# Experts in sorted order with 192, 128 or 64 slots, and 64-slot blocks whose high and low parts share one tile

## The chip, the cores and the metric

One core of one Trainium2 chip runs the whole program. The metric is device time in microseconds (us) of that core for one execution.

## The reference, cut to what matters

Two layers work on 256 latent tokens (and 256 context tokens) of 1024 channels. The second layer ends with a mixture of eight experts, and only that part is touched here:

```python
def moe_swiglu(h, router, w1, w3, w2):
    logits = (h @ router).astype(jnp.float32)
    top_v, top_i = lax.top_k(logits, TOP_K)            # 2 of 8
    top_w = jax.nn.softmax(top_v, axis=-1)
    ...
    out = comb[..., 0:1] * swiglu(h, w1[0], w3[0], w2[0])
    for e in range(1, N_EXPERTS):
        out = out + comb[..., e:e + 1] * swiglu(h, w1[e], w3[e], w2[e])
    return out

def swiglu(h, w1, w3, w2):
    return (jax.nn.silu(h @ w1) * (h @ w3)) @ w2
```

All is float32. w1 and w3 of an expert are 1024 x 3584, w2 is 3584 x 1024. Each of the 256 tokens goes to two experts, so the eight experts have 512 tokens in all. On the reference's default inputs the router gives them 39, 31, 9, 142, 44, 100, 55 and 92 tokens.

## The kernel before

**Precision.** The tensor engine's one-pass float32 format holds part of a float32 number. `split` (lines 116 to 124) makes of a tile a high part `h` (a cast on ScalarE, line 120) and the rest `lo` (a subtraction on VectorE, line 121); `mm3` (lines 126 to 130) then multiplies in three passes, high x high, high x low and low x high, which accumulate in PSUM.

**Positions.** `route` (lines 966 to 1091) finds the two experts of each token and the rank of each token within its expert. The expert with the most tokens is position 0 of an order, and the others follow cyclically by number (lines 1022 to 1040). Position 0 has 256 slots in two blocks, the seven others have one block of 128 slots. What is beyond 128 tokens of an expert other than position 0 is handled after the rest by overflow positions 8 and 9 (two at most), under a condition on the chip (lines 1297 to 1301).

**A block.** `gather` (lines 1093 to 1120) builds one-hot rows and takes the block's tokens with matmuls from `hm`, which holds the tokens split: result are two tiles `xg` (high and low), tokens as columns. Then come seven chunks of 512 hidden units. `up1` (line 1147) multiplies by a chunk of w1 and applies silu on ScalarE; `up3` (line 1154) multiplies by a chunk of w3, takes the product on VectorE (line 1159), transposes it with four matmuls against the identity (line 1162) and splits it (line 1164) into `gh` and `gl`; `down` (line 1168) multiplies these by the chunk of w2 and accumulates 128 x 1024 results `y`. The block of tokens is the stationary operand of all these matmuls, and 512 columns of weights move. `back` (line 1172) adds the block's results, weighted, to the rows of its tokens.

**Weights.** `mload` (line 1122) loads 1 MB of weights from SP's queue into one of five buffers `mland` and splits it in two pieces into `mwh` and `mwl` (eight buffers each). A chunk takes six such loads, an expert 42.

**Order.** `steps` (line 1211) runs positions 1 to 7, three steps a chunk: `up1`, the `down` of the chunk before, `up3`. The other generator, `steps0` (line 1248), runs both blocks of position 0 on the same weights, two steps a chunk: `up1`, and `up3` with `down`, whose results are added up in SBUF (lines 1264, 1266). `experts` (line 1269) interleaves them: after two steps of the first and then after every tenth, one of the 14 steps of position 0. The next position's gather is made at a position's chunk 5. A scheduler then puts the instructions of each engine in order, by priorities and its own estimate of times, so that matmuls of neighbouring steps can be mixed. PSUM has three banks for `mp` (and gathers and results), four for `y`, and one for transposes.

Of the kernel before, what the change touches and what calls it, by code (L numbers as in the profile page):

```python
# [10 lines left out]
FT = mybir.dt.float32  # L11
# [8 lines left out]
KD = 8  # L20
# [6 lines left out]
MAGIC = 12582912.0  # L27
INV2PI = 1.0 / (2.0 * math.pi)
# [17 lines left out]
def tables():  # L46
# [24 lines left out]
    for i in range(8):  # L71
        for tp in range(8):
            for ch in range(16):
# [3 lines left out]
                if k <= 0:  # L77
# [3 lines left out]
    c["moec"] = np.broadcast_to(np.concatenate([i8, np.mod(i8[None, :] - i8[:, None], 8).ravel(),  # L81
                                                np.arange(128)]).astype(f32), (128, 200)).copy()
# [5 lines left out]
class Net:  # L88
# [43 lines left out]
    def wchunk(self, src, n, tags=None):  # L132
        """One weight chunk of 512 KB, split: its n blocks of columns."""
# [66 lines left out]
    def s5_pre(self, l):  # L200
# [54 lines left out]
        for b in range(NB):  # L255
# [24 lines left out]
            def cmul(o, va, vb, vc, op1, eng):  # L280
                """(ar * va op0 ai * vb, ar * vc op1 ai * va), products over powers and channels."""
# [187 lines left out]
    def hy_filters(self, l):  # L469
        """Transforms of both orders' two-sided filters (over 256) to DRAM."""  # L470
# [62 lines left out]
    def hy_in(self, l, t0, part):  # L533
        """Short convolution of one part of the projection."""
# [15 lines left out]
    def hy_turn(self, q, s, out):  # L550
        """Token-major copy of a part of one sequence; two tiles get its split."""
# [11 lines left out]
    def hy_conv(self, kk, z, order, sink):  # L563
        """Long convolution of one sequence; sink takes each piece of the result."""
# [59 lines left out]
    def hy_second(self, l, z1, x1, seqs):  # L624
        """The second order; the result takes the place of x1."""
# [69 lines left out]
    def stats(self, x):  # L695
        """Mean, (var + eps)^-0.5 and -mean times that of the rows of a token tile."""
# [16 lines left out]
    def norm_affine(self, out, x, g, b):  # L713
        """Layer norm of a token tile with the rows g, b."""
# [12 lines left out]
    def modulate(self, xn, w, sh, sc):  # L727
        """Two normalized token tiles (w: context or latent) transposed, modulated and split into hh, hl."""
# [21 lines left out]
    def mods(self, l, part, tag="Y", fast=False):  # L750
        """Part 0..5 of the modulation (shift, scale, gate, twice) as columns [128, tile, (context, latent)]; the
# [779 lines left out]
```

## Time and profile before

| | |
|---|---|
| median of 3 runs | 2717.94 us (2716.2 to 2720.52) |
| profiled execution, first to last instruction (span) | 2714.0 us |
| mean granted TensorE clock over the span | 0.956 |
| tensor engine busy | 2542.4 us, 94% |
| VectorE, ScalarE, GpSimd busy | 2191.7, 1384.9, 191.3 us |
| DMA | 602.58 MB, mean 222 GB/s |
| expert stage | from about 1565 us to the end |

The profile was taken of one execution; its own time is known as its span, 2714.0 us, which is 3.9 us under the runs' median. Busy time of an engine is a share of the span over all stages. A matmul's shown duration includes its way through the array and overlaps those beside it; the distance between two starts is what it costs in a dense stream. The granted clock is that of the tensor engine, 1.00 being 2.4 GHz and 0.50 being 1.2 GHz.

### The profile page before, as it was taken

How to read it: one execution, taken by the hardware profiler on the slowest of the kernel's cores; microseconds unless marked ns; L12 is line 12 of the kernel's file. 1: busy time of each engine (PE TensorE's matmuls, PEld its weight loads, DVE VectorE, ACT ScalarE, POOL GpSimd, SP SyncE). 2: the span in 40 equal slices, each digit the busy share in tenths (PEclk: the TensorE clock that was granted, in tenths of full speed). 3: DMA queues.
4: the chain of work that ended last, by engine and by line, in shares of the span. 5: the costliest groups of instructions: out<-in, count | busy, mean ns of one | idle time of the engine just before them, and what ended most of it. 6: DMA issues, size and time to landing. Idle time of an engine off the chain costs nothing. (4 is left out here: it accounts for less than half of the span.)

```text
span 2714.0 us, 35372 instructions
## 1 busy us (share of the span) xinstructions
PE 2542.4 (94%) x12732; PEld 2117.1 (78%) x12732; DVE 2191.7 (81%) x3154; ACT 1384.9 (51%) x1891; POOL 191.3 (7%) x202
## 2 busy tenths in 40 slices
PE   7888999999899989969999799999999999999997
PEld 3766886788777878858999688888888888888875
DVE  8876799975769897566898787888878788888887
ACT  4344442333542323334445376777767676777764
POOL 2520010000100132110000100000000000000000
PEclk8988999999899989979899889999999999999998
DMA  6454444533235555545445288898889898898974
GB/s 254 152 190 152 144 126 168 179 130 113 79 126 189 179 187 170 189 149 187 152 148 175 89 328 307 324 342 310 329 292 332 295 334 302 322 337 318 334 270 177
DMA packets 147353, 602.58 MB, mean 222 GB/s; under 512 B 41878, under 2 KB 42584, under 8 KB 104160
## 3 DMA queue, kind: packets, MB, share of 16 engines
q1 hardware_dynamic: 147168, 600.23, 62.9%
q8 instruction: 102, 1.67, 0.2%
q14 instruction: 83, 0.68, 0.1%
HBM read 563.96 MB, written 36.21 MB: 221 GB/s over the span
## 5 line engine op out<-in xcount | busy, mean ns | idle before, releaser
L121 DVE TENSOR_TENSOR mwl<-mland,mwh 128x1024 fp32r<-128x1024 f32 x672 | 802.9, 1221 | 157.8 <-ACT mwh L120 133.4
L120 ACT CAST mwh<-mland 128x1024 fp32r<-128x1024 f32 x672 | 700.3, 1054 | 276.6 <-PE mp L130 188.9
L120 ACT CAST wh<-land 128x512 fp32r<-128x512 f32 x396 | 244.7, 621 | 527.7 <-PE p L129 242.0
L128 PE MATMUL mp<-mwh,xg 128*128 128x512 f32 x1008 | 395.7, 394 | 0.4 <-ACT xg L1113 0.4
L129 PE MATMUL mp<-mwl,xg 128*128 128x512 f32 x1008 | 395.2, 392 | 0.0
L130 PE MATMUL mp<-mwh,xg 128*128 128x512 f32 x1008 | 394.7, 392 | 0.0
L121 DVE TENSOR_TENSOR wl<-land,wh 128x512 fp32r<-128x512 f32 x396 | 285.0, 723 | 114.8 <-ACT wh L120 106.4
L128 PE MATMUL p<-hh,wh 128*128 128x256 f32 (+1 forms) x800 | 278.5, 349 | 14.2 <-DVE q L546 8.1
L130 PE MATMUL p<-hh,wl 128*128 128x256 f32 (+1 forms) x800 | 278.6, 350 | 4.6 <-DVE wl L121 3.9
L129 PE MATMUL p<-hl,wh 128*128 128x256 f32 (+1 forms) x800 | 276.0, 346 | 0.1
L130 PEld LDWEIGHTS mp<-mwh,xg 128*128 128x128 f32 x1008 | 189.9, 188 | 39.6
L128 PEld LDWEIGHTS mp<-mwh,xg 128*128 128x128 f32 x1008 | 189.9, 189 | 39.0 <-ACT xg L1113 0.5
L129 PEld LDWEIGHTS mp<-mwl,xg 128*128 128x128 f32 x1008 | 190.1, 189 | 38.4
L128 PE MATMUL y<-mwh,gh 128*128 128x512 f32 x504 | 195.9, 391 | 1.8 <-ACT gh L120 1.8
L129 PE MATMUL y<-mwl,gh 128*128 128x512 f32 x504 | 196.0, 390 | 0.0
L130 PE MATMUL y<-mwh,gl 128*128 128x512 f32 x504 | 190.1, 392 | 0.0
L128 PEld LDWEIGHTS p<-hh,wh 128*128 128x128 f32 x800 | 157.6, 197 | 34.4 <-issue 8.7
L784 DVE SCALAR_TENSOR_TENSOR ma<-mw,sv,ma 128x512 f32<-128x512 f32 x196 | 153.1, 804 | 37.0 <-DMA mw<-in_w_mod 36.5
L130 PEld LDWEIGHTS p<-hh,wl 128*128 128x128 f32 x800 | 157.3, 197 | 25.8 <-DVE wl L121 8.9
L129 PEld LDWEIGHTS p<-hl,wh 128*128 128x128 f32 x800 | 158.0, 198 | 15.9 <-DVE hl L748 0.3
L130 PE MATMUL fo<-hh,wl 128*128 128x512 f32 (+1 forms) x384 | 147.2, 384 | 2.7 <-DVE wl L121 2.7
L128 PE MATMUL fo<-hh,wh 128*128 128x512 f32 (+1 forms) x384 | 147.5, 385 | 1.4 <-ACT hh L744 0.9
(442 smaller groups left out, 4369.8 us busy)
## 6 DMA issues: line engine op xcount, KB each, us to landing
mland<-in_moe_w SPq DMA_DIRECT2D x336, 1024.0 KB, 6.3
mw<-in_w_mod SPq DMA_DIRECT2D x96, 512.0 KB, 3.5
land<-in_w_in SPq DMA_DIRECT2D x96, 512.0 KB, 3.7
land<-in_ffn_w SPq DMA_DIRECT2D x66, 512.0 KB, 3.6
land<-in_w_bo SPq DMA_DIRECT2D x24, 512.0 KB, 3.5
s5we<-weT SPq DMA_DIRECT2D x16, 512.0 KB, 3.9
s5wc<-sw SPq DMA_DIRECT2D x16, 512.0 KB, 2.9
we<-s5we SPq DMA_DIRECT2D x16, 512.0 KB, 5.7
```

What stands on the lines that cost most here:

```text
L120: nc.scalar.copy(h, src)
L121: nc.vector.tensor_sub(lo, src, h.bitcast(FT))
L128: nc.tensor.matmul(o, a[0], b[0], start=start, stop=False)
L129: nc.tensor.matmul(o, a[0], b[1], start=False, stop=False)
L130: nc.tensor.matmul(o, a[1], b[0], start=False, stop=stop)
L784: nc.vector.scalar_tensor_tensor(ac[:, t], wk, self.sv[:, k, t:t + 1], ac[:, t], op0=OP.mult, op1=OP.add)
```

## The change

Positions are now sorted by token count, most first, and the slots go by position: 192 for position 0 (a block of 128 and one of 64), 128 for positions 1 to 3, 64 for positions 4 to 7. Overflow blocks (128 slots, up to three, any position) run afterwards where an expert has more tokens than slots.

A block of 64 slots ("light": block 1 of position 0, and positions 4 to 7) has one tile `xg`, with the high parts of its 64 tokens in columns 0 to 63 and the low parts in columns 64 to 127. `mmx` multiplies it in two passes, by the high and by the low part of the weights, where a block of 128 slots takes the three of `mm3`. The sum of the upper and lower 64 rows is then the product. `up1` and `up3` copy the two projections out of PSUM; eight float32 matmuls against `fold` (two 64 x 64 identities, one over the other) transpose them and add their halves; then come silu, product and split, at 256 elements a partition instead of 512. The down-projection's halves are added in `back`, whose one-hot rows are there twice. Positions 1 to 7 run in the order 1, 4, 2, 5, 3, 6, 7, and the 14 steps of position 0 go into positions 4 and 5 (five each), 6 (three) and 7 (one). The buffers of `ms` and `ms0` become one pool of five; `oh` and `ohf` have one buffer instead of two.

```diff
+CAPS = (192, 128, 128, 128, 64, 64, 64, 64)
+NOV = 3
+NMS = 5
...
     def route(self, xr):
...
-        cm = sm.tile([128, 1], FT, name="cm", tag="cm", bufs=1)
-        nc.vector.tensor_reduce(cm, cnt, axis=mybir.AxisListType.X, op=OP.max)
-        nc.vector.tensor_scalar(eq, cnt, cm, None, op0=OP.is_equal)
-        es = sm.tile([128, 1], FT, name="es", tag="es", bufs=1)
-        self.first(es, eq, i8, 8.0)
...
+        mine, other = cnt[:, :, None].to_broadcast(P), cnt[:, None, :].to_broadcast(P)
+        nc.vector.tensor_tensor(pm, other, mine, op=OP.is_equal)
+        nc.vector.tensor_mul(pm, pm, low)
+        nc.vector.tensor_tensor(pt, other, mine, op=OP.is_gt)
+        nc.vector.tensor_add(pt, pt, pm)
+        nc.vector.tensor_reduce(eq, pt, axis=mybir.AxisListType.X, op=OP.add)
+        nc.vector.tensor_tensor(pm, eq[:, None, :].to_broadcast(P), i8[:, :, None].to_broadcast(P), op=OP.is_equal)
+        reorder(od[:, :8], i8)
...
         def rest():
...
-            for j in range(2):
+            for j in range(NOV):
...
-    def gather(self, pos, b):
+    def gather(self, pos, b=0):
...
-        oh = p.tile([128, 2, 128], FR, name="oh", tag="oh", bufs=2)
-        ohf = p.tile([128, 2, 128], FT, name="ohf", tag="ohf", bufs=2)
+        light = b == 1 or 4 <= pos < 8
+        oh = p.tile([128, 2, 128], FR, name="oh", tag="oh", bufs=1)
+        ohf = p.tile([128, 2, 128], FT, name="ohf", tag="ohf", bufs=1)
...
-        for r in range(2):
-            xg = p.tile([128, KD, 128], FR, name=f"xg{r}", tag="xg", bufs=8)
+        for parts in ((0, 1),) if light else ((0,), (1,)):
+            xg = p.tile([128, KD, 128], FR, name=f"xg{parts[0]}", tag="xg", bufs=8)
+            m = 128 // len(parts)
             for q in range(2):
                 o = self.psum.tile([128, 512], FT, name="xgp", tag="mm", bufs=3)
                 for kk in range(4):
...
+                    for i, r in enumerate(parts):
+                        for a in range(2):
+                            nc.tensor.matmul(o[:, kk * 128 + i * m:kk * 128 + (i + 1) * m],
+                                             self.hm[:, r, a, k * 128:(k + 1) * 128],
+                                             oh[:, a, :m], start=a == 0, stop=a == 1)
...
+    def mmx(self, o, x, i, w, start, stop):
+
+        if len(x) == 2:
+            self.mm3(o, (x[0][:, i], x[1][:, i]), w, start, stop)
+        else:
+            for r in range(2):
+                self.nc.tensor.matmul(o, x[0][:, i], w[r], start=start and r == 0, stop=stop and r == 1)
...
-    def up1(self, e, ch, xgs, tag, bufs):
+    def up1(self, e, ch, xgs):
+
         pr = []
...
+            if len(xg) == 2:
+                self.nc.scalar.activation(pr[-1], ps, AF.Silu)
+            else:
+                self.nc.scalar.copy(pr[-1], ps)
...
     def up3(self, e, ch, xgs, pr):
...
+            else:
+                p3 = p.tile([128, 512], FT, name="ms3", tag="ms", bufs=NMS)
+                nc.scalar.copy(p3, ps)
+                tp = self.psum.tile([128, 512], FT, name="gtp", tag="tr", bufs=1)
+                for i, t in enumerate((pb, p3)):
+                    for f in range(4):
+                        nc.tensor.matmul(tp[:, i * 256 + f * 64:i * 256 + (f + 1) * 64], t[:, f * 128:(f + 1) * 128],
+                                         self.fold, start=True, stop=True)
+                h = p3[:, :256]
+                nc.scalar.activation(h, tp[:, :256], AF.Silu)
+                nc.vector.tensor_mul(h, h, tp[:, 256:])
+                self.split(g[0][:, :, :64], g[0][:, :, 64:], h.rearrange("p (f s) -> p f s", f=4))
...
     def experts(self, rest):
...
+        order = (1, 4, 2, 5, 3, 6, 7)
+        turns = [21 * i + d for i, ds in ((1, (1, 5, 9, 13, 17)), (3, (1, 5, 9, 13, 17)), (5, (1, 7, 13)), (6, (4,)))
+                 for d in ds]
...
-                if n0 < 14 and n >= 2 + 10 * n0:
+                if n in turns:
                     next(first)
...
-            nov = nc.values_load(self.ovi[0:1, 2:3], min_val=0, max_val=2)
-            with tc.If(nov >= 1):
...
+            nov = nc.values_load(self.ovi[0:1, NOV:NOV + 1], min_val=0, max_val=NOV)
+            with ExitStack() as es:
+                for j in range(NOV):
+                    es.enter_context(tc.If(nov >= j + 1))
+                    self.run(self.steps([(8 + j, load(self.ovi, j), self.gather(8 + j))]))
```

## Rows read from the trace of the kernel before

**Rows 1.** The page, part 1: busy time, share of the span, instructions.

```profile
PE 2542.4 (94%) x12732; PEld 2117.1 (78%) x12732; DVE 2191.7 (81%) x3154; ACT 1384.9 (51%) x1891; POOL 191.3 (7%) x202
```

**Rows 2.** Groups by line and shape, 1568 to 2714 us: busy us, mean ns, idle before.

```profile
L121 DVE TENSOR_TENSOR mwl<-mland,mwh 128x1024 fp32r<-128x1024 f32 x672 | 802.9, 1221 | 157.8 <-ACT mwh L120 133.4 <-PE y L130 3.1
L120 ACT CAST mwh<-mland 128x1024 fp32r<-128x1024 f32 x672 | 700.3, 1054 | 276.6 <-PE mp L130 188.9 <-PE y L130 76.3 <-DMA mland<-in_moe_w 2.7
L128 PE MATMUL mp<-mwh,xg 128*128 128x512 f32 x1008 | 395.7, 394 | 0.4 <-ACT xg L1113 0.4
...
L128 PE MATMUL y<-mwh,gh 128*128 128x512 f32 x504 | 195.9, 391 | 1.8 <-ACT gh L120 1.8
...
L1162 PE MATMUL gtp<-ident,ms 128*128 128x128 f32 x252 | 38.5, 274 | 4.9 <-DVE ms L1159 4.9
...
L1194 DVE SCALAR_TENSOR_TENSOR macc<-yo,cbp,macc 128x512 f32<-128x512 f32 x32 | 22.9, 744 | 3.1 <-PE yo L1188 3.1
```

**Rows 3.** Stretches: length, busy us (count) of PE, PEld, DVE, ACT, POOL; PEclk, DMA share, GB/s.

```profile
1573.00:1600.00 27.00, 26.76 (x146) 23.27 (x147) 24.41 (x41) 24.55 (x35) 0.00 (x0) 0.94 1.02 415
1600.00:2600.00 1000.00, 996.88 (x4600) 826.88 (x4599) 828.21 (x793) 708.12 (x768) 0.00 (x0) 1.00 0.87 319
2600.00:2690.00 90.00, 85.15 (x376) 67.99 (x376) 75.62 (x77) 56.22 (x63) 0.00 (x0) 0.98 0.70 256
```

**Rows 4.** Timeline of PE, matmuls of one chunk: start us, us, instruction.

```profile
1620.80 0.39 PE L128 MATMUL mp<-mwh,xg 128*128 128x512 f32 x1
...
1626.25 0.60 PE L1162 MATMUL gtp<-ident,ms 128*128 128x128 f32 x4
1626.60 0.48 PE L128 MATMUL mp<-mwh,xg 128*128 128x512 f32 x1
1626.92 0.40 PE L129 MATMUL mp<-mwl,xg 128*128 128x512 f32 x1
```

**Rows 5.** Timeline of PE, an earlier stage, plain float32 matmuls of 64 columns.

```profile
1330.12 2.00 PE L381 MATMUL ep<-U,we 128*128 128x64 f32 x16
```

**Rows 6.** Timeline of DVE, back to back.

```profile
1700.00 2.35 DVE L121 TENSOR_TENSOR mwl<-mland,mwh 128x1024 fp32r<-128x1024 f32 x2
1702.27 0.16 DVE L1099 TENSOR_SCALAR rk<-rkp 128x2 f32<-128x2 f32 x1
...
1744.09 0.68 DVE L121 TENSOR_TENSOR yL<-y,yH 128x512 fp32r<-128x512 f32 x1
1744.69 4.69 DVE L121 TENSOR_TENSOR mwl<-mland,mwh 128x1024 fp32r<-128x1024 f32 x4
```

**Rows 7.** Groups of DVE and ACT over the span, 256 elements a partition.

```profile
L748 DVE TENSOR_TENSOR hl<-f,hh 128x256 fp32r<-128x256 f32 x48 | 18.0, 413 | 3.5 <-ACT hh L742 3.5
...
L742 ACT CAST hh<-f 128x256 fp32r<-128x256 f32 x24 | 9.3, 407 | 0.1
```

**Rows 8.** DMA issues, 1560 to 2714 us: KB each, median us to landing.

```profile
mland<-in_moe_w SPq DMA_DIRECT2D x336, 1024.0 KB, 6.3
```

**Rows 9.** Stretches as in rows 3: the stage's start, then a steady stretch.

```profile
1580.00:1588.00 8.00, 8.00 (x49) 7.02 (x48) 6.37 (x13) 6.87 (x10) 0.00 (x0) 1.00 1.02 426
...
1612.00:1670.00 58.00, 58.00 (x263) 47.99 (x262) 50.25 (x46) 43.57 (x46) 0.00 (x0) 1.00 0.92 346
```

**Rows 10.** Waits, 1573 to 2690 us: us in total, times, longest.

```profile
ACT mwh L120 <- PE mp L130: 188.9, 307, 5.1
DVE mwl L121 <- ACT mwh L120: 133.4, 124, 3.9
```

**Rows 11.** Timeline at the stage's end.

```profile
2686.36 0.39 PE L130 MATMUL mp<-mwh,xg 128*128 128x512 f32 x1
2686.78 0.69 DVE L1159 TENSOR_TENSOR ms<-ms,mp 128x512 f32<-128x512 f32 x1 [2.90 <-PE mp L130]
...
2688.22 0.59 ACT L120 CAST gh<-gtp 128x512 fp32r<-128x512 f32 x1 [5.59 <-PE gtp L1162]
...
2688.86 0.50 PE L128 MATMUL y<-mwh,gh 128*128 128x512 f32 x1 [0.67 <-ACT gh L120]
```

More of the change, by code (lines that the diff above doesn't have):

```diff
@@ L1060, in route @@
             nc.sync.dma_start(self.xm[:, a], xr[2 + a])
-        self.iota = sm.tile([128, 128], FT, name="iota", tag="hsw", bufs=1)
-        nc.vector.tensor_copy(self.iota, mc[:, 72:200])
+        iota = sm.tile([128, 136], FT, name="iota", tag="hsw", bufs=1)
+        nc.vector.tensor_copy(iota, mc[:, 72:208])
+        caps, self.iota = iota[:, :8], iota[:, 8:136]
         def rest():
@@ L1100, in gather @@
         for a in range(2):
-            nc.vector.tensor_scalar(ohf[:, a], self.iota, rk[:, a:a + 1], None, op0=OP.is_equal)
+            m = 64 if light else 128
+            for c in range(0, 128, m):
+                nc.vector.tensor_scalar(ohf[:, a, c:c + m], self.iota[:, :m], rk[:, a:a + 1], None, op0=OP.is_equal)
         nc.scalar.copy(oh, ohf)
         xs = []
-        for r in range(2):
-            xg = p.tile([128, KD, 128], FR, name=f"xg{r}", tag="xg", bufs=8)
+        for parts in ((0, 1),) if light else ((0,), (1,)):
+            xg = p.tile([128, KD, 128], FR, name=f"xg{parts[0]}", tag="xg", bufs=8)
+            m = 128 // len(parts)
             for q in range(2):
@@ L1108, in gather @@
                 for kk in range(4):
-                    for a in range(2):
-                        k = 4 * q + kk
-                        nc.tensor.matmul(o[:, kk * 128:(kk + 1) * 128], self.hm[:, r, a, k * 128:(k + 1) * 128],
-                                         oh[:, a], start=a == 0, stop=a == 1)
+                    k = 4 * q + kk
+                    for i, r in enumerate(parts):
+                        for a in range(2):
+                            nc.tensor.matmul(o[:, kk * 128 + i * m:kk * 128 + (i + 1) * m],
+                                             self.hm[:, r, a, k * 128:(k + 1) * 128],
+                                             oh[:, a, :m], start=a == 0, stop=a == 1)
                 nc.scalar.copy(xg[:, 4 * q:4 * q + 4].rearrange("p k s -> p (k s)"), o)
@@ L1169, in down @@
         c = slice(h * 512, (h + 1) * 512)
-        self.mm3(y, (g[0][:, f], g[1][:, f]), [a[:, c] for a in w[f - 2 * q]], start, stop)
+        self.mmx(y, g, f, [a[:, c] for a in w[f - 2 * q]], start, stop)
     def back(self, pos, y, ot, first=False):
@@ L1282, in then @@
             def then(pos):
-                if pos < 7:
-                    g[pos + 1] = self.gather(pos + 1, 0)
-            n0 = 0
-            for n, _ in enumerate(self.steps(((pos, load(self.odi, pos), g.pop(pos)) for pos in range(1, 8)), then)):
+                if pos != order[-1]:
+                    nxt = order[order.index(pos) + 1]
+                    g[nxt] = self.gather(nxt)
+            for n, _ in enumerate(self.steps(((pos, load(self.odi, pos), g.pop(pos)) for pos in order), then)):
                 self.pump()
@@ L1296, in experts @@
             self.pump(1000)
-            nov = nc.values_load(self.ovi[0:1, 2:3], min_val=0, max_val=2)
-            with tc.If(nov >= 1):
-                self.run(self.steps([(8, load(self.ovi, 0), self.gather(8, 1))]))
-                with tc.If(nov >= 2):
-                    self.run(self.steps([(9, load(self.ovi, 1), self.gather(9, 1))]))
+            nov = nc.values_load(self.ovi[0:1, NOV:NOV + 1], min_val=0, max_val=NOV)
[3 more added lines that the diff above has]
+                    self.run(self.steps([(8 + j, load(self.ovi, j), self.gather(8 + j))]))
     def store_x(self, dst, xr, nts):
```

69 lines of the change are left out of this document (34 added, 35 removed).

## The prediction

> **What bounds the kernel now.** I began with the page's engine line: the tensor engine (PE) is busy for 94% of the span and the vector engine (DVE) for 81% [rows 1]. That is a mean over stages, and the change touches only the expert stage, so I asked for that stage by stretches: over its middle 1000 us PE is busy 996.9 us, DVE 828 and ScalarE (ACT) 708, and the DMA engines 0.87 [rows 3]. So PE has no idle time there that a transfer or a split could be blamed for. The waits say the same: ACT, which makes the high parts of the weights, waits 188.9 us for PE to give a buffer back, and DVE waits 133.4 us for ACT behind it [rows 10]. The suppliers wait for PE, and PE for nobody. Time comes out of this stage by giving PE less to do, until DVE, ACT or the loads set the pace.
>
> What PE does: 1008 x 3 matmuls of the two up-projections and 504 x 3 of the down-projection [rows 2] (one line of three each), 4536 of 512 columns, or 72 for each of 7 chunks of 9 blocks. In the timeline 24 of them take 1626.25 - 1620.80 = 5.45 us, 0.227 us each [rows 4]; the 0.39 us shown for one overlaps its neighbours and isn't its price. 4536 x 0.227 = 1030 us of the 1117 between 1573 and 2690 us.
>
> **Part 1, fewer passes.** A 64-slot block holds high and low parts of its tokens side by side as one stationary tile, so a product takes two matmuls, not three. Five blocks become light (second half of the first position, positions 4 to 7). Per chunk a light block has 48 matmuls, not 72: 24 x 0.227 = 5.45 us less. 5 blocks x 7 chunks = 35: **-190.8 us**. All of it lies on PE, the bound. Four heavy blocks stay as they were.
>
> **Part 2, the fold.** In place of 4 transposes a light chunk has 8 plain float32 matmuls, with 64 columns moving. A transpose group costs 0.35 us to the next start, and the next matmul comes 0.10 us late: 0.45 us [rows 4]. The nearest row for the fold is the earlier stage's float32 product of 64 columns: 16 records take 2.00 us [rows 5], and that line calls 8 matmuls a group, so a call makes two records. Eight folds are thus such a group; less the last record's own 0.25 us of overlap, plus 0.10, I take 1.85 us. The bounds are 1.4 us (16 records at the 0.35 / 4 of a transpose) and 2.1 (the whole 2.00 and the late start). 1.85 - 0.45 = 1.40 more, x 35: **+49 us**, bounds +33 to +58. The net of both parts is -141.8 us.
>
> **Part 3, the other engines.** The loads stay at 336 of 1 MB [rows 8], and so do the 672 pairs of casts and subtractions. Back to back a DVE subtraction costs 1.135 us and a 512-wide one 0.60 [rows 6]. A light chunk's product and subtraction shrink to 256 elements, 0.41 us for 0.68 [rows 7, 11]: DVE loses some 19 us of its 928 (the sum over [rows 3]) and is then busy for about 909 in a stage of 990, 92%. ACT gets two 512-wide copies and two 256-wide operations (2 x 0.59 + 2 x 0.41) for two 512-wide ones: +0.8 us x 35 = 28 us, on an engine that was 71% busy. Both costs are hidden under PE as long as the stretch is PE-bound, which the new order decides. A light chunk alone costs PE 48 x 0.227 + 1.85 = 12.8 us, but DVE 12 x 1.135 + 0.7 = 14.3, so on its own it is DVE-bound. A chunk of the first position costs PE 27.2 + 0.45 + 1.85 = 29.5 and DVE some 18. With the five half-steps of the first position in each of positions 4 and 5, PE needs 7 x 12.8 + 2.5 x 29.5 = 163 and DVE 145: PE-bound. Position 6 has 1.5 such chunks (134 to 127), still PE. Position 7 has half a chunk, early: from there on some 5.3 chunks take PE 68 + 7 us (results of three blocks, a row), DVE 76 + 18; the split buffers hold 3 to 4 loads ahead, 8 us. So PE starves there: **+11 us**, bounds 0 and +31 (all of DVE's excess, and no lead).
>
> **Part 4, the longer chain.** From the last up-matmul to the first down-matmul, the chain was product, transposes, cast: with nothing else to do at the stage's end it took 2.5 us [rows 11]. In a light chunk it is copy 0.59, folds 1.85, silu, product, cast, subtraction at 0.41 each; PE is idle for 2.2 us of it if nothing covers it, and four of its links queue in order behind splits of 1.05 (ACT) or 1.2 us (DVE) [rows 2], at most 5.6 us more. What covers it is the next chunk's first projection, now 16 x 0.227 = 3.6 us, and a step of the first position where there is one. Before, the cover was so good that PE waited 1.8 + 4.9 us in all for this chain [rows 2]. Lower bound 0.1 us a chunk (that row), upper 2.2 + 5.6 = 7.8. With half of the queueing it is 5.0 against 3.6 of cover, 1.4 exposed. I take 0.5 us, nearer to the first since the order interleaves steps as before: **+17 us**.
>
> **Part 5, small edits.** Sorting replaces the search for the fullest expert: nine small DVE operations for ten, before the first weights; the third overflow entry adds some 17 of 0.16 us [rows 6] among the first splits, and one-hot buffers go from two to one, which delays the second gather at the start: **+2 us** together, bounds 0 and +5. Gathers have 32 matmuls for light and heavy blocks alike: nothing. SP issues the same loads in the same chunks; the load of an expert's number comes once for each position as before; POOL has nothing in the stage.
>
> **Sum.** -141.8 + 11 + 17 + 2 = -112 us on a span of 2714.0: 2602. The runs' median lies 3.9 us above the span, which I add: **2606 us**.
>
> **Rivals.** *The loads set the pace.* 352.3 MB must come in some 990 us, 356 GB/s, where the middle of the stage had 319 [rows 3]. For it: in the steady stretch 346 GB/s took 0.92 of the DMA engines, which is 376 at full share [rows 9], and a heavy chunk at 16.8 us already needs 375. Against it: 426 GB/s at the stage's start [rows 9]. At 376 a load takes 2.79 us: position 7 gets 45 x 2.79 = 126 against 113 for PE, position 6 142 against 139, and hitches in the heavy positions cost some 5 us: 2616. If the stage could draw no more than its 319, the loads would need 1104 us and hardly anything would be won: 2705. Chance 0.12 of being over 2620 for this reason.
>
> The Trainium skill (DMA: Bandwidth & Descriptors, section "Where 436 GB/s comes from") says that of transfers from HBM the limit of a core's share, about 358 GB/s, binds. The 426 of this case's trace stands above it; by 358, as an estimate, a load takes 2.93 us, positions 6 and 7 lose 29 us rather than 11, and the sum would be 2624.
>
> *The chain comes bare (slower).* In each light chunk ACT's queue holds a weight cast that waits for PE's buffer ahead of the chain's copy or silu, and PE runs dry before the down-projection. It decides from 129 / 35 = 3.7 us idle a chunk; with all queueing and no cover it is 7.8 us: 2606 - 17 + 273 = 2862. For it speaks ACT's longest wait for a buffer, 5.1 us [rows 10]; against it, that PE can run the next projection meanwhile. Half bare, at 1.4 us, gives 2638. Chance 0.02 for the slower end, 0.04 for 2640 to 2710.
>
> *The slots don't hold the tokens.* The reference's router on its default inputs sends 142, 100, 92, 55, 44, 39, 31 and 9 tokens to the experts, sorted, and the slots are 192, 128 x 3, 64 x 4: no overflow block runs. With other inputs each would add 42 loads with little beside them, some 125 us: 2731. Chance 0.02.
>
> **The numbers.** The forecast has 0.80. Its own range is 2576 (no stall of parts 3 and 4, 2606 less 28) to 2640; I reach to 2660 for half of the loads' and the chain's cases, and to 2574 below. What this kernel's measurement can tell from no change is 0.2%, 5 us. Faster: all but the bare chain, the overflow and the worst of the loads, 0.95; same 0.02; slower 0.03.
>
> **What would show it.** 3696 matmuls of 512 columns, at 0.227; 35 x 16 fold records at some 0.11 us; the stage shorter by about 112 us; 336 loads. DVE over 90%, and ACT's wait for PE's buffers much shorter. PE idle in the last 70 us of the stage with DVE unbroken (part 3), elsewhere under 2%. I'm wrong if PE is idle by tens of us in positions 4 and 5, if the fold takes much over 2 us, or if the DMA share stands at 1.0 while splits wait for loads.

## The result and the profile after

| | before | after |
|---|---|---|
| median of 4 runs, taken in turns | 2718.76 us (2716.2 to 2720.52) | 2629.46 us (2621.37 to 2638.14) |
| ratio, 95% interval | | 0.9676 (0.965 to 0.9701) |
| profiled execution, span | 2714.0 us | 2636.3 us |
| router's first matmul | 1547.5 us | 1563.3 us |
| from there to the end ("the stage" below) | 1166.5 us | 1073.0 us |
| DMA | 602.58 MB | 602.52 MB |

The change saves 89 us by the medians. The forecast was 2606, the range 2574 to 2660: direction and range held, and the forecast was 23 us too low. The profiled execution of after is the slowest of its four runs, so its time is best compared from the router's first matmul on: everything ahead of it is not touched by the change, and the traces show the same instructions in the same order there. From there the stage lost 93.5 us; the sum had said 112.

The page of after, part 1 (to be read against [rows 1]):

```profile
PE 2435.7 (92%) x12312; PEld 2029.3 (77%) x12312; DVE 2162.4 (82%) x3182; ACT 1373.0 (52%) x1951; POOL 191.5 (7%) x202
```

Groups of after by line and shape, 1568 to 2636 us (columns as in [rows 2]):

```profile
L124 DVE TENSOR_TENSOR mwl<-mland,mwh 128x1024 fp32r<-128x1024 f32 x672 | 788.6, 1220 | 79.1 <-ACT mwh L123 65.6 <-PE mp L1154 6.1 <-PE y L133 1.2
L123 ACT CAST mwh<-mland 128x1024 fp32r<-128x1024 f32 x672 | 675.2, 1052 | 122.6 <-PE mp L133 37.0 <-PE mp L1154 29.2 <-PE y L1154 25.5
L1154 PE MATMUL mp<-mwl,xg 128*128 128x512 f32 x560 | 223.9, 402 | 5.2 <-DVE mwl L124 5.1
...
L131 PE MATMUL mp<-mwh,xg 128*128 128x512 f32 x448 | 178.0, 397 | 2.6 <-ACT mwh L123 2.6
...
L1154 PE MATMUL y<-mwh,gh 128*128 128x512 f32 x280 | 112.5, 410 | 8.1 <-DVE gh L124 8.1
...
L1197 PE MATMUL gtp<-fold,ms 128*128 128x64 f32 x560 | 71.8, 269 | 7.9 <-DVE ms L1201 3.4 <-ACT ms L1176 1.7 <-DVE gl L124 1.5
...
L1189 PE MATMUL gtp<-ident,ms 128*128 128x128 f32 x112 | 16.9, 273 | 0.0
```

Line 1154 is the two-pass product (`mmx`), lines 131 to 133 are the three-pass one. Two lines of 560 and 280 and three of 448 and 224 make 3696 matmuls of 512 columns, as worked out, in place of 4536. The fold is 560 records, 35 x 16, as worked out. Now look at the idle time: before, PE waited for nobody [rows 2]; now it waits for casts, subtractions and the parts of the chain. And ACT's wait for PE's buffers is down from 188.9 us [rows 10] to 37.0 + 29.2 for the same kind of buffer.

Stretches of before over its stage, and of after (columns as in [rows 3]):

```profile
1576.00:2400.00 824.00, 820.89 (x3819) 681.98 (x3818) 682.34 (x666) 589.51 (x648) 0.00 (x0) 1.00 0.87 321
2400.00:2690.00 290.00, 285.14 (x1297) 233.98 (x1296) 242.89 (x237) 196.37 (x212) 0.00 (x0) 0.99 0.83 302
```

```profile
1592.00:1800.00 208.00, 203.99 (x995) 170.50 (x994) 184.78 (x212) 160.39 (x188) 0.00 (x0) 1.00 0.94 354
1800.00:2400.00 600.00, 587.83 (x2796) 488.51 (x2796) 521.00 (x526) 452.51 (x535) 0.00 (x0) 0.99 0.92 344
2400.00:2612.00 212.00, 192.78 (x911) 156.36 (x911) 190.57 (x194) 161.35 (x199) 0.00 (x0) 0.95 0.88 337
```

Before, PE was idle for 824 + 290 - 820.9 - 285.1 = 8.0 us; after, for 1020 - 984.6 = 35.4. The idle time itself is close to what the forecast allowed. What it had not allowed for is the column of the granted clock: 0.95 over the last 212 us, 0.99 over 600. A mean of c over a stretch of t us stands for 2 x (1 - c) x t us at 1.2 GHz: 21 + 12 = 33 us after, and 6 before. These rows are rounded; the same column read every 2 us gives 33.5 after and 3.7 before. Times at 1.2 GHz below are read in this way.

Where such a dip begins is seen in the timeline of PE, after, after a light chunk's two up-projections (start us, us, instruction, idle before):

```profile
2362.30 0.40 PE L1154 MATMUL mp<-mwl,xg 128*128 128x512 f32 x1
2363.38 1.10 PE L1197 MATMUL gtp<-fold,ms 128*128 128x64 f32 x8 [0.68 <-ACT ms L1176]
2367.05 0.80 PE L1154 MATMUL y<-mwh,gh 128*128 128x512 f32 x1 [2.57 <-DVE gh L124]
2367.65 0.63 PE L1154 MATMUL y<-mwl,gh 128*128 128x512 f32 x1
2368.07 0.63 PE L1154 MATMUL y<-mwh,gh 128*128 128x512 f32 x1
...
2370.21 0.41 PE L1154 MATMUL y<-mwl,gh 128*128 128x512 f32 x1
```

PE waits 0.68 us for the copy and 2.57 us for the chain's last subtraction, and then its matmuls follow one another every 0.43 us instead of every 0.23, until about 2370. So the stall is paid nearly one and a half times: 3.25 us idle, and some 7 matmuls at 0.2 us more, 1.4 us.

The Trainium skill (TensorE: Matmul & The Clock Gate, "Why this matters for your kernels") says that idle gaps between bursts of matmuls bring the engine back to its lower clock. This trace agrees, with these 3.25 us in two parts and the slower matmuls behind them.

Two more places show who is late. The timeline of all engines, after, at 2413 us (ACT's queue) and at 2562 us (DVE's):

```profile
2413.22 0.39 ACT L1200 ACTIVATE ms<-gtp 128x256 f32<-128x256 f32 x1 [1.13 <-PE gtp L1197]
...
2413.91 0.59 ACT L1176 COPY ms<-mp 128x512 f32<-128x512 f32 x1 [0.31 <-PE mp L1154]
2414.39 2.00 ACT L123 CAST mwh<-mland 128x1024 fp32r<-128x1024 f32 x2
...
2415.49 0.50 PE L1154 MATMUL mp<-mwh,xg 128*128 128x512 f32 x1 [1.62 <-ACT mwh L123]
```

```profile
2562.02 1.22 DVE L1244 SCALAR_TENSOR_TENSOR macc<-macc 128x1024 f32<-128x1024 f32 x1
...
2562.82 1.00 PE L1197 MATMUL gtp<-fold,ms 128*128 128x64 f32 x8
2563.15 6.90 DVE L124 TENSOR_TENSOR mwl<-mland,mwh 128x1024 fp32r<-128x1024 f32 x6
...
2566.70 0.50 PE L1154 MATMUL mp<-mwl,xg 128*128 128x512 f32 x1 [2.59 <-DVE mwl L124]
```

In the first, ACT waits 1.13 us for the fold ahead of its silu, and the weight cast that PE needs next stands behind it in ACT's queue: an added wait, and what is queued behind it. In the second, DVE did operations of 1.22 us for the residual (lines 1243, 1244) between its splits, has six splits to catch up, and PE waits 2.59 us for the first of them that it needs.

### The profile page after: what moved, and what is told of

It reads as the page before. It is cut to its first block, busy times and chain, and to the rows that moved or that the text cites. A ratio compares the mean times of both kernels' runs of the same rounds, so it can differ in the third digit from the quotient of the medians.

```text
span 2636.3 us, 34684 instructions
## 1 busy us (share of the span) xinstructions
PE 2435.7 (92%) x12312; PEld 2029.3 (77%) x12312; DVE 2162.4 (82%) x3182; ACT 1373.0 (52%) x1951; POOL 191.5 (7%) x202
## 2 busy tenths in 40 slices
DMA packets 147349, 602.52 MB, mean 229 GB/s; under 512 B 41878, under 2 KB 42584, under 8 KB 104160
## 5 line engine op out<-in xcount | busy, mean ns | idle before, releaser
L124 DVE TENSOR_TENSOR mwl<-mland,mwh 128x1024 fp32r<-128x1024 f32 x672 | 788.6, 1220 | 79.1 <-ACT mwh L123 65.6
L123 ACT CAST mwh<-mland 128x1024 fp32r<-128x1024 f32 x672 | 675.2, 1052 | 122.6 <-PE mp L133 37.0
L1154 PE MATMUL mp<-mwl,xg 128*128 128x512 f32 x560 | 223.9, 402 | 5.2 <-DVE mwl L124 5.1
L1154 PE MATMUL mp<-mwh,xg 128*128 128x512 f32 x560 | 221.2, 397 | 3.5 <-ACT mwh L123 2.8
L131 PE MATMUL mp<-mwh,xg 128*128 128x512 f32 x448 | 178.0, 397 | 2.6 <-ACT mwh L123 2.6
L132 PE MATMUL mp<-mwl,xg 128*128 128x512 f32 x448 | 177.7, 397 | 1.7 <-DVE mwl L124 1.6
L133 PE MATMUL mp<-mwh,xg 128*128 128x512 f32 x448 | 176.4, 394 | 0.0
L132 PE MATMUL fo<-hl,wh 128*128 128x512 f32 (+1 forms) x384 | 146.1, 381 | 0.1
L669 DVE SCALAR_TENSOR_TENSOR dc<-ub,cfp,dc 128x512 f32<-128x512 f32 (+1 forms) x240 | 142.9, 622 | 0.6
L1154 PEld LDWEIGHTS mp<-mwl,xg 128*128 128x128 f32 x560 | 106.5, 190 | 30.9 <-DVE mwl L124 10.3
L1154 PEld LDWEIGHTS mp<-mwh,xg 128*128 128x128 f32 x560 | 106.5, 190 | 24.7 <-ACT mwh L123 4.6
```

Source lines behind the costliest of these rows:

```text
L123: nc.scalar.copy(h, src)
L124: nc.vector.tensor_sub(lo, src, h.bitcast(FT))
L131: nc.tensor.matmul(o, a[0], b[0], start=start, stop=False)
L132: nc.tensor.matmul(o, a[0], b[1], start=False, stop=False)
L133: nc.tensor.matmul(o, a[1], b[0], start=False, stop=stop)
L669: nc.vector.scalar_tensor_tensor(d, ub[:, :R, i:i + 64], cfp[:, j, i:i + 1], d, op0=OP.mult, op1=OP.add)
```

## Experiments

All times are of the stage (router's first matmul to the end of the span), unless said otherwise, and of one profiled execution each. Before has 1166.5, after 1073.0. An edit also lets the scheduler order the instructions anew: in every edited kernel the order on PE, DVE or ACT differs from that of the kernel it is compared with, and no run separates this part of a figure.

**The same kernels again.**

> The kernel before, unchanged, for a second trace. The changed kernel's trace reaches the router's first matmul at 1563.3 us where the kernel before reached it at 1547.5, although every engine runs the same instructions in the same order up to there. If that 16 us is the granted clock differing from one execution to the next, whichever the kernel: the router's first matmul lies anywhere between 1545 and 1565 us here and in the next run, and from there to the end it takes 1166 us again, within 3. If the change itself slows the early part: 1547.5 here again, within 2.

> The changed kernel, unchanged. If the early 16 us are the clock's: the router's first matmul before 1560 us in this trace, total some 2615 to 2630. If the change slows the early part: 1563 again. From the router's first matmul to the end 1073 us again, within 6: there the stalls and the half-clock stretches behind them vary a little.

Measured: before 1166.6, after 1071.0; medians 2711.93 and 2626.51, ratio 0.9676 (0.9656 to 0.9697). The stage repeats within 2 us. The part ahead of it doesn't: it took 1547.5 and 1548.1 us in before and 1563.3 and 1553.5 in after. That is why the experiments are compared by their stage. For that part, 1553.5 in after speaks for the first reading; 1548.1 in before fits both.

**Without the light blocks.** Sorting, order and turns stay; every block has two tiles and three passes.

```diff
-        light = b == 1 or 4 <= pos < 8
+        light = False
```

> The changed kernel with every block treated as one of 128 slots: three passes, transposes and no fold, with the sorted order and the new turns kept. If the gain comes from the passes alone: the 4536 matmuls are back and it takes 1160 to 1172 us from the router's first matmul to the end (1166.5 before). If sorting, order or buffers brought part of it: under 1155. If sorting and the new turns cost something that the passes paid for: over 1175.

Measured: 1169.2 (total 2722.65, before in the same runs 2722.3). Its stretches:

```profile
1580.00:2400.00 820.00, 817.03 (x3788) 679.09 (x3787) 678.33 (x685) 584.48 (x641) 0.00 (x0) 1.00 0.87 320
2400.00:2696.00 296.00, 291.23 (x1326) 240.44 (x1325) 248.21 (x240) 203.47 (x219) 0.00 (x0) 0.99 0.82 302
```

These are the rows of before but for 3 us. The whole gain is in the two passes; sorting and the new order save nothing by themselves.

**With the old order and turns**, and the light blocks kept.

```diff
-        order = (1, 4, 2, 5, 3, 6, 7)
-        turns = [21 * i + d for i, ds in ((1, (1, 5, 9, 13, 17)), (3, (1, 5, 9, 13, 17)), (5, (1, 7, 13)), (6, (4,)))
-                 for d in ds]
+        order = (1, 2, 3, 4, 5, 6, 7)
+        turns = [2 + 10 * i for i in range(14)]
```

> The changed kernel with the positions in their own order, 1 to 7, and a step of the first position after every tenth step, as the kernel before has it. Positions 4 to 7 then have one chunk of the first position each, 119 us of PE's work against some 118 of VectorE's and, at 376 GB/s, 134 of the loads'. If the loads at that rate bind in light positions: 1110 to 1130 us from the router's first matmul to the end. If only VectorE and the chain bind: 1075 to 1090. If the order is worth nothing: 1073.

Measured: 1088.3, 15 us more than after. Its stretches:

```profile
1592.00:2100.00 508.00, 504.94 (x2379) 420.40 (x2379) 434.44 (x442) 376.56 (x422) 0.00 (x0) 1.00 0.89 331
2100.00:2600.00 500.00, 465.92 (x2190) 380.98 (x2189) 439.20 (x451) 379.78 (x470) 0.00 (x0) 0.95 0.93 350
```

Now the first half is nearly full on PE, and the second, where the light positions stand together, leaves PE idle for 34 us, at a DMA share of 0.93. Order and turns together are worth 15 us, not the 37 to 57 us that loads at 376 GB/s would have cost here.

**Half of each load.** Each load is 0.5 MB, and what it brings is split twice, in the place of two pieces.

```diff
-        w = p.tile([128, 2048], FT, name="mland", tag="mland", bufs=5)
-        nc.sync.dma_start(w, src)
+        w = p.tile([128, 1024], FT, name="mland", tag="mland", bufs=5)
+        nc.sync.dma_start(w, src[:, :1024])
...
-            self.split(h, lo, w[:, q * 1024:(q + 1) * 1024])
+            self.split(h, lo, w)
```

> The changed kernel with each load half as long (the second half of each weight piece is not loaded; the first half is split twice in its place), so DMA traffic of the stage is halved and every other engine's work is the same. Theory (PE's 32 us of new idle come from ACT and DVE: starved splits and the chain): from the router's first matmul to the end 1065 to 1075 us, no change. Rival (the loads set the pace in light positions): the idle goes and the clock stays up, 1030 to 1050.

**Half of the subtractions.** Of each load one low part is made, and used for both halves. (The eight buffers `mwl` then last for twice as many loads.)

```diff
-            lo = p.tile([128, 1024], FR, name="mwl", tag="mwl", bufs=8)
-            self.split(h, lo, w[:, q * 1024:(q + 1) * 1024])
+            nc.scalar.copy(h, w[:, q * 1024:(q + 1) * 1024])
+            if q == 0:
+                lo = p.tile([128, 1024], FR, name="mwl", tag="mwl", bufs=8)
+                nc.vector.tensor_sub(lo, w[:, :1024], h.bitcast(FT))
```

> The changed kernel with half of the weights' subtractions left out on VectorE (the second half of each load takes the low part of the first), so VectorE has some 380 us less work in the stage. Theory (VectorE's share of the starving): from the router's first matmul to the end 1035 to 1055 us. Rival (loads or ACT set the pace): 1068 to 1075.

Measured: 1047.5 with half loads, 1045.4 with half the subtractions (some 3 us of this second figure are a router that ran at a higher clock, ahead of the first weights). Their stretches from 1800 us on, half loads first:

```profile
1800.00:2400.00 600.00, 594.81 (x2859) 495.50 (x2858) 536.85 (x541) 470.22 (x552) 0.00 (x0) 1.00 0.60 177
2400.00:2584.00 184.00, 172.37 (x834) 140.06 (x834) 171.50 (x178) 144.67 (x181) 0.00 (x0) 0.98 0.60 181
```

```profile
1800.00:2400.00 600.00, 589.98 (x2835) 492.76 (x2834) 315.97 (x337) 456.64 (x544) 0.00 (x0) 0.99 0.92 349
2400.00:2584.00 184.00, 174.32 (x851) 143.34 (x849) 111.17 (x121) 146.42 (x183) 0.00 (x0) 0.98 0.88 353
```

Either supplier, halved, removes the same 25 us: PE's idle time falls from 35.4 us to 18 and 22, and the clock of the last part rises from 0.95 to 0.98. For DVE that is what the theory of the starving tail said. For the loads I had expected no change, and that fell: 1047.5 lies in the rival's range, though only half of the idle time went. Both stand in one line: a landing buffer is free for the next load when ACT and DVE have read it (in after the queue of the loads waited 676 us in all for DVE's subtractions), so a late DVE makes a late load and a load that takes less time gives DVE its piece sooner. How much is the loads' own isn't settled: in after ACT waited 7.9 us in all for a load, with half loads 3.0, and with the smaller tile the scheduler also put the instructions into another order, ACT's from the first casts on. Even with half of either, the last stretch keeps 10 to 12 us of idle time, which halving one of them alone doesn't take away.

**The fold twice.** Each fold matmul is done twice into the same sum.

```diff
-                        nc.tensor.matmul(tp[:, i * 256 + f * 64:i * 256 + (f + 1) * 64], t[:, f * 128:(f + 1) * 128],
-                                         self.fold, start=True, stop=True)
+                        for z in range(2):
+                            nc.tensor.matmul(tp[:, i * 256 + f * 64:i * 256 + (f + 1) * 64],
+                                             t[:, f * 128:(f + 1) * 128], self.fold, start=z == 0, stop=z == 1)
```

> Every fold matmul runs twice (the sum is doubled in the light blocks), 16 more records in each of 35 light chunks. If PE's time is the bound all through: 35 x 1.8 = +63 us from the router's first matmul to the end, 1134 to 1137. If the light stretches have slack on PE that the suppliers set: only +25 to +45, 1097 to 1118.

Measured: 1097.9, 24.9 us more. The group of the folds, and the stretches of this kernel:

```profile
L1198 PE MATMUL gtp<-fold,ms 128*128 128x64 f32 x1120 | 134.5, 271 | 1.0 <-ACT ms L1176 0.7 <-DVE gl L124 0.2
```

```profile
1800.00:2400.00 600.00, 597.90 (x3036) 506.45 (x3035) 515.44 (x518) 447.41 (x526) 0.00 (x0) 1.00 0.91 339
2400.00:2620.00 220.00, 211.59 (x1119) 179.96 (x1118) 190.76 (x195) 161.71 (x199) 0.00 (x0) 0.97 0.85 323
```

PE got 134.5 - 71.8 = 62.7 us more to do by busy time, or 35 x 2 x 0.81 = 57 by the distance of starts (0.81 us for 8 records, 2562.82 to 2563.63 us in after), and the stage grew by 24.9. So in after PE has slack beside the light chunks: what it is given fills its idle time (10.5 us in these two stretches, in after 31.4) and keeps the clock up (1.00 and 0.97 for 0.99 and 0.95). Once passes are gone, a microsecond of PE's in a light chunk is worth some 0.4.

**A short chain.** In the light chunks the split reads the fold's result.

```diff
-                h = p3[:, :256]
-                nc.scalar.activation(h, tp[:, :256], AF.Silu)
-                nc.vector.tensor_mul(h, h, tp[:, 256:])
-                self.split(g[0][:, :, :64], g[0][:, :, 64:], h.rearrange("p (f s) -> p f s", f=4))
+                self.split(g[0][:, :, :64], g[0][:, :, 64:], tp[:, :256].rearrange("p (f s) -> p f s", f=4))
```

> In light blocks silu and the product are left out, so that two links of the chain are gone (0.4 us on ACT, 0.4 us on VectorE a chunk, 28 us in all of work that is not PE's) and the folded tile is split straight from PSUM. Theory (the light chunks lose PE time to the chain's links in ACT's and VectorE's queues): 1050 to 1062 us from the router's first matmul to the end. Rival (the loads set the pace): 1069 to 1074.

Measured: 1060.8, 12 us less. The removed work is 35 x 0.41 us on DVE and as much on ACT, neither of which is the bound over the stage: part of the idle time is the chain's, or that of the work left out; this run doesn't tell the two apart. The clock of its last stretch (2400 to 2590 us) is 0.98.

**Later turns.** The last steps of position 0 are kept for positions 6 and 7.

```diff
-        turns = [21 * i + d for i, ds in ((1, (1, 5, 9, 13, 17)), (3, (1, 5, 9, 13, 17)), (5, (1, 7, 13)), (6, (4,)))
+        turns = [21 * i + d for i, ds in ((1, (1, 6, 11, 16)), (3, (1, 6, 11, 16)), (5, (1, 8, 15)), (6, (1, 6, 11)))
```

> The 14 steps of the first position put later: four in each of positions 4 and 5, three each in 6 and 7 (the change has 5, 5, 3, 1). Every light position then has 134 to 149 us of PE work against 127 to 136 of VectorE's. Theory (in the light stretches without steps of the first position PE starves on splits, which half the loads or half the subtractions showed to cost 25 us together with the clock): from the router's first matmul to the end 1055 to 1064 us against 1071 and 1073. Rival (the stalls come from the chain and from ACT's queue order in every light chunk, wherever the steps are): 1068 to 1075.

Measured: 1067.6, 5 us less, just under the rival's range; median 2623.44, ratio 0.967 (0.9639 to 0.9702), not to be told from after's. If a lack of PE work in position 7 were all that starved PE, two more half-steps of 15 us there would have freed most of it. From the cast of that position's first load to the stage's last chain, in after and then here:

```profile
2459.00:2612.00 153.00, 136.74 (x625) 109.65 (x624) 138.39 (x144) 112.41 (x139) 0.00 (x0) 0.94 0.85 326
```

```profile
2418.50:2592.40 173.90, 161.90 (x762) 132.93 (x760) 156.44 (x163) 126.00 (x157) 0.00 (x0) 0.96 0.85 322
```

PE was idle there for 16.3 us in after and still for 12.0 with the later turns. With half of the subtractions it was 7.6 (135.7 us from 2439 us on, 128.1 busy): DVE's work is a part of it. That the order of single instructions makes the rest is argued, not shown.

The next three start from this kernel.

**Nine split buffers** in place of eight, for a longer lead.

```diff
-            h = p.tile([128, 1024], FR, name="mwh", tag="mwh", bufs=8)
-            lo = p.tile([128, 1024], FR, name="mwl", tag="mwl", bufs=8)
+            h = p.tile([128, 1024], FR, name="mwh", tag="mwh", bufs=9)
+            lo = p.tile([128, 1024], FR, name="mwl", tag="mwl", bufs=9)
...
-            xg = p.tile([128, KD, 128], FR, name=f"xg{parts[0]}", tag="xg", bufs=8)
+            xg = p.tile([128, KD, 128], FR, name=f"xg{parts[0]}", tag="xg", bufs=7)
```

(the room comes from one `xg`, one `gl`, and `fold` in the place of another constant)

> The kernel with later turns, and nine instead of eight buffers for the pieces of split weights (room made by seven xg buffers, two gl buffers and the fold matrix in a constant's place). Theory (PE starves when the suppliers' lead of a few loads is used up between steps of the first position): 1055 to 1063 us from the router's first matmul to the end, against 1067.6 with eight. Rival (ACT's and VectorE's queue order makes the stalls, whatever the lead): 1065 to 1070.

Measured: 1072.6, 5 us more than later_turns and above both ranges, nearer the rival's. PE's idle time from the first matmul on weights to the last chain is the same (33.1 us for 33.7), and 37 us in place of 28 went by at 1.2 GHz. A longer lead brought nothing that shows; but the edit also took an `xg` and a `gl` away, so that lead is worth nothing isn't shown.

**Work of DVE on GpSimd**: the light chunks' subtraction, and the residual's operations.

```diff
-                self.split(g[0][:, :, :64], g[0][:, :, 64:], h.rearrange("p (f s) -> p f s", f=4))
+                h3 = h.rearrange("p (f s) -> p f s", f=4)
+                nc.scalar.copy(g[0][:, :, :64], h3)
+                nc.gpsimd.tensor_sub(g[0][:, :, 64:], h3, g[0][:, :, :64].bitcast(FT))
...
-            nc.vector.tensor_mul(self.acc[:, a], self.acc[:, a], self.g2)
-            nc.vector.scalar_tensor_tensor(self.acc[:, a], y0[:, a], ALPHA, self.acc[:, a],
-                                           op0=OP.mult, op1=OP.add)
+            nc.gpsimd.tensor_mul(self.acc[:, a], self.acc[:, a], self.g2)
+            nc.scalar.mul(y0[:, a], y0[:, a], ALPHA)
+            nc.gpsimd.tensor_add(self.acc[:, a], self.acc[:, a], y0[:, a])
```

> The kernel with later turns, and some 20 us of VectorE's work in the stage given to GpSimd, which is idle there: the light blocks' subtraction of 256 elements (35 of them) and the residual's four operations of 1024. Theory (VectorE, late with splits behind such operations, is one of PE's suppliers in the light stretches and at the end): 1055 to 1064 us from the router's first matmul to the end, against 1067.6. Rivals: GpSimd's longer operation lengthens the chain by as much as it takes out of VectorE's queue, 1065 to 1072; the two engines disturb one another, over 1072.

Measured: 1091.4, 24 us more than later_turns. This is the range of the rival in which the two engines disturb one another, and the trace shows that they do. The moved subtraction (shortest, median and longest ns), then DVE's subtractions of weights in later_turns and here:

```profile
L1204 POOL TENSOR_TENSOR gh<-ms,gh x35: 722/1397/6414, 1737.9 to 2622.7; 128x256 fp32r<-128x256 f32 x35
```

```profile
L124 DVE TENSOR_TENSOR mwl<-mland,mwh x672: 1209/1218/1228, 1573.3 to 2590.7; 128x1024 fp32r<-128x1024 f32 x168
```

```profile
L124 DVE TENSOR_TENSOR mwl<-mland,mwh x672: 1209/1221/3449, 1581.8 to 2620.6; 128x1024 fp32r<-128x1024 f32 x168
```

Timelines of POOL and of DVE in this kernel, at three places:

```profile
1814.18 6.41 POOL L1204 TENSOR_TENSOR gh<-ms,gh 128x256 fp32r<-128x256 f32 x1 [10.36 <-ACT gh L1203]
1813.11 6.89 DVE L124 TENSOR_TENSOR mwl<-mland,mwh 128x1024 fp32r<-128x1024 f32 x6
...
2609.52 6.70 POOL L1247 TENSOR_TENSOR macc<-macc 128x1024 f32<-128x1024 f32 x2
2604.91 16.93 DVE L124 TENSOR_TENSOR mwl<-mland,mwh 128x1024 fp32r<-128x1024 f32 x8 [2.38 <-ACT mwh L123]
...
2622.69 0.72 POOL L1204 TENSOR_TENSOR gh<-ms,gh 128x256 fp32r<-128x256 f32 x1 [6.47 <-ACT gh L1203]
```

Where DVE does nothing (2622.69 us), the subtraction takes 0.72 us on GpSimd, for 0.42 on DVE. Beside six of DVE's subtractions it lasts 6.41 us, about as long as these. Beside GpSimd's operations for the residual, eight of DVE's subtractions take 16.9 us in place of 9.1 (8 x 1.135). PE's group at the chain's end, in later_turns and here:

```profile
L1154 PE MATMUL y<-mwh,gh 128*128 128x512 f32 x280 | 111.0, 402 | 2.7 <-DVE gh L124 1.9 <-ACT mwh L123 0.9
```

```profile
L1154 PE MATMUL y<-mwh,gh 128*128 128x512 f32 x280 | 118.2, 429 | 20.2 <-POOL gh L1204 19.2 <-ACT mwh L123 1.0
```

PE waits 19.2 us for the moved link, for 1.9 in later_turns. Over the stage it is idle for 43.3 us in place of 33.7, and 62 us in place of 28 go by at 1.2 GHz. The run doesn't give the price of a link: the longer chain and DVE's slower splits come together in it.

**The first projection folded early.** If the chain is what PE waits for, what can leave it should: the first projection's copy, fold and silu need not wait for the second.

```diff
+    def foldm(self, t):
+        tp = self.psum.tile([128, 512], FT, name="gtp", tag="tr", bufs=1)
+        for f in range(4):
+            self.nc.tensor.matmul(tp[:, f * 64:(f + 1) * 64], t[:, f * 128:(f + 1) * 128], self.fold,
+                                  start=True, stop=True)
+        return tp
...
                 self.nc.scalar.copy(pr[-1], ps)
+                tp = self.foldm(pr[-1])
+                self.nc.scalar.activation(pr[-1][:, :256], tp[:, :256], AF.Silu)
...
                 nc.scalar.copy(p3, ps)
...
-                nc.scalar.activation(h, tp[:, :256], AF.Silu)
-                nc.vector.tensor_mul(h, h, tp[:, 256:])
+                tp = self.foldm(p3)
+                h = pb[:, :256]
+                nc.vector.tensor_mul(h, h, tp[:, :256])
```

> The kernel with later turns, and in light blocks the first projection folded and put through silu as soon as it is done, so that after the second projection only its copy, four folds, the product, the cast and the subtraction are left: one link of ACT's and four folds (0.9 us) less in the chain, with the same operations in all. Two links less, and their work, gave 10 to 12 us in the short chain; 1.5 us more of it a chunk, on GpSimd, cost 24. Theory (the length of the chain between the projections and the down-projection sets PE's idle in light chunks): 1050 to 1060 us from the router's first matmul to the end, against 1067.6; total 2603 to 2620. Rival (it was the work left out on ACT and VectorE that helped in the short chain, not its length): 1065 to 1070. Rival (folds in two groups hold the one transposition bank twice, and stop PE twice): over 1070.

Measured: 1053.7, 14 us less than later_turns and 19 less than after; median of 5 runs 2608.0 (2602.89 to 2614.22), ratio to before 0.9596 (0.957 to 0.9623): below after's 0.965 to 0.9701, so this beats both kernels. Two groups of PE, in later_turns (its group at the chain's end stands above) and here:

```profile
L131 PE MATMUL mp<-mwh,xg 128*128 128x512 f32 x448 | 178.7, 399 | 6.0 <-ACT mwh L123 6.0
```

```profile
L131 PE MATMUL mp<-mwh,xg 128*128 128x512 f32 x448 | 178.0, 397 | 1.6 <-ACT mwh L123 1.6
...
L1154 PE MATMUL y<-mwh,gh 128*128 128x512 f32 x280 | 109.8, 402 | 3.7 <-DVE gh L124 3.7
```

The time lies in the theory's range, but the gain isn't at the chain's end: PE waits there for 3.7 us, for 1.9 in later_turns (8.1 in after). What fell is PE's waiting for split weights in the heavy blocks, 6.0 to 1.6 us for casts and 4.5 to 1.6 for subtractions. In all PE was idle for 27.1 us in place of 33.7, and 18 us in place of 28 went by at 1.2 GHz. No work was removed. So moving work ahead in the two queues helped; that the chain's length was the reason isn't shown.

## Why the prediction was right, and where it was not

**The bound** (right). PE was the bound and paid for every pass: without the light blocks nothing is gained, 1169.2 for 1166.5.

**Part 1, -190.8** (right). 3696 matmuls were forecast and seen, and where nothing is late they follow one another every 0.23 us (2407.78 to 2408.01 us in the timeline of after), as before. All of it came off PE; not all of it came off the end.

**Part 2, +49** (right). The trace has 71.8 / 35 = 2.05 us of a light chunk's folds for 16.9 / 28 = 0.60 of a heavy chunk's transposes: 1.45 x 35 = +51. From start to start, the half of a fold (8 records) takes 0.81 us (2562.82 to 2563.63), two of them 1.62 and with a late start of 0.1 each 1.8; I had taken 1.85.

**Parts 3 and 4, +28 for PE's idle time** (right in sum and by place, the cause in part). It grew by 27 us, 8.0 to 35.4. Part 3 is about position 7: from the cast of its first load on, PE was idle for 16.3 us after, and before for 4.9 (167 us from 2523 us on, 162.2 busy), +11, where part 3 had 11. Ahead of that it went from 3.1 to 19.1, +16, where part 4 had 17. But the causes aren't two separate ones: that the tail starves for DVE alone fell with the later turns, which left 12.0 of the 16.3 us, and with half of the subtractions, which left 7.6. DVE was neither unbroken nor busy for over 90%: 896 of 1020 us, 88%, with 65.6 us of waiting for ACT over the stage. And outside the last 70 us PE was idle for 24 of 950 us, 2.5%, where the prediction had under 2%. What the timelines point to, and no run separates, is the chain's links standing in the two queues that also carry the splits: either a link is late behind a split, or a split behind a link's wait. Two bounds of the prediction don't follow from its own terms: all of DVE's excess in position 7 is 94 - 75 = 19 us, not 31, and 2606 less 28 is 2578, not 2576. The forecast doesn't rest on them.

**The step that was missing: the clock.** Each stall of part 3 and 4 was priced as idle time alone. The rows show 33.5 us at 1.2 GHz for 3.7 before. A matmul takes 0.43 us there for 0.23, so of each such microsecond 0.47 is lost: 30 x 0.47 = **+14 us**, which no term held. With it the sum is -190.8 + 51 + 27 + 14 = -99 for 93.5 measured; 5 us aren't placed. Every experiment that took idle time away had a higher clock in the last stretch too (0.98 with half of a supplier and with a short chain, for 0.95), so stall and dip go together. The account holds for the other runs: in each kernel with as many matmuls and folds as after, what is left of the time from the first matmul on weights to the last chain, less PE's idle time and 0.47 of the time at 1.2 GHz, is between 965 and 972 us (after: 969; before: 1104).

**Part 5, +2** (nearly nothing). From the router's first matmul to the first matmul on weights takes 25.7 us in both.

**From the span to the median.** 18 of the profiled execution's 34 us over the forecast are the stage's (112 for 93.5); 16 are the part ahead of it, which the change doesn't touch. That part, before and after:

```profile
0.00:1547.50 1547.50, 1409.59 (x7509) 1177.63 (x7510) 1234.90 (x2114) 590.01 (x1018) 187.75 (x198) 0.94 0.48 159
```

```profile
0.00:1563.30 1563.30, 1424.02 (x7509) 1190.28 (x7510) 1234.19 (x2114) 589.92 (x1018) 187.91 (x198) 0.93 0.48 157
```

The same 7509 matmuls kept PE busy for 14.4 us longer, at a granted clock of 0.93 for 0.94: most of the 16 us is the clock's. Over twelve executions of changed kernels the start of the stage lies between 1545.5 and 1563.3 us, at the same work: with the change it can be as early as before, or 16 us later. In before it varies as well: the spans of its other runs, less 1166.5 us, put it between 1542 and 1560. But in each of the four comparisons by medians, less the stage, it comes 4 to 9 us later in the changed kernel. This is an estimate, since the stage is known for profiled executions alone; by it some 5 of the forecast's 23 us lie ahead of the stage. What lowers the clock there stays open.

**The rivals.** *Loads set the pace*: it gave 2616 or more, which the time doesn't tell from the forecast; its price does. With light positions side by side, where it would have cost 37 to 57 us, 15 were seen, and in after ACT waited 7.9 us for loads. A stretch of after has 365 GB/s at a share of 0.95, close to the 376 that I had taken for a full share:

```profile
2400.00:2500.00 100.00, 93.72 (x457) 76.95 (x457) 90.25 (x90) 81.59 (x100) 0.00 (x0) 0.98 0.95 365
```

So the loads are near their limit but don't set the pace alone; halving them does remove 25 us, and what of this is theirs isn't settled.

The Trainium skill (DMA: Bandwidth & Descriptors, "Where 436 GB/s comes from") has about 358 GB/s as the binding limit of a core's share from HBM. The 365 of this stretch stands above it, over 100 us.

*The chain comes bare*: PE waited 8.1 us in all for the chain's last link, and was idle for 35.4 us for all reasons, against 129 (3.7 a chunk) needed to undo the gain. The mechanism is there, at a fraction of its price. *Slots overflow*: 336 loads, none for an overflow.

## What to carry to other kernels

Taking work from the bound pays in full only until the suppliers' queues become the next bound: here, of 191 us of PE's work, 51 went into the fold and some 40 came back as stalls and a lower clock. Price a stall of the tensor engine with the slower matmuls behind it, not by its length alone. When an added chain runs in the queues of engines that also feed the bound, first move ahead what isn't needed at its end (14 us here, for no work less), and don't put one of its links on GpSimd while DVE subtracts: here the two held one another up, and it cost 24 us.

## What the runs showed of the hardware

- The clock also fell behind short stalls: here of 1.18 and 0.77 us, with the granted clock at 0.50 and matmuls every 0.43 us behind them. Timeline of PE, after:

```profile
1925.43 0.49 PE L131 MATMUL mp<-mwh,xg 128*128 128x512 f32 x1 [1.18 <-ACT mwh L123]
1926.69 0.80 PE L132 MATMUL mp<-mwl,xg 128*128 128x512 f32 x1 [0.77 <-DVE mwl L124]
1927.28 0.63 PE L133 MATMUL mp<-mwh,xg 128*128 128x512 f32 x1
...
1929.84 0.44 PE L132 MATMUL y<-mwl,gh 128*128 128x512 f32 x1
```

- GpSimd and DVE held one another up where both took two operands from SBUF: GpSimd's subtraction of 256 elements a partition took 0.72 us where DVE did nothing and 6.41 beside six of DVE's subtractions, and DVE's took up to 3.45 us beside GpSimd's operations of 1024, for 1.22 without. A mean over a group, 1.88 us for this subtraction, hides that.
- A plain float32 matmul has two records, and a group of four with 64 columns took 0.81 us to the next start, 0.10 a record.
